# A two-layer decoder trunk: one plain pair of up-projections a layer in place of two, right factors at four steps a chunk, three buffers of weight parts, bias read later

## The chip, the cores and the metric

The kernel runs on one core of a Trainium2 chip. The metric is the device time of one execution in microseconds (us); lower is better. Names of engines in profiles: PE is TensorE, with PEld its weight loads; DVE is VectorE, ACT is ScalarE, POOL is GpSimd, and SP is SyncE, which issues the reads of weights. L345 is line 345 of the kernel.

## The reference

Input and output are 512 tokens by 1024 channels in float32. Layer 0 is a causal convolution module followed by a SwiGLU feed-forward network (FFN). After it keys and values are projected once. Layer 1 is sliding-window attention with a relative-position bias and its own FFN, and a last RMSNorm. The FFN, D_FF = 2816, is the larger part of the work:

```python
def rmsnorm(x, g):
    xf = x.astype(jnp.float32)
    xf = xf * lax.rsqrt(jnp.mean(xf * xf, axis=-1, keepdims=True) + EPS)
    return (xf * g.astype(jnp.float32)).astype(x.dtype)

def swiglu_ffn(x, w_up, w_down):
    gate, up = jnp.split(x @ w_up, 2, axis=-1)
    return (jax.nn.silu(gate) * up) @ w_down
```

## The kernel before

**Products.** Every float32 product is made from two shorter parts of each factor, a high half and a low half, with three matmuls (`mm3`): high by high (L345), high weights by the low half of the activation (L346), low weights by the high half (L347). `h[0..7]` holds the residual stream, 128 channels by 512 tokens in each tile.

**Weights.** They are read in chunks of 512 KB (128x1024) on SP's queue into four `raw` buffers, in the order of a list, `PLAN`, and up to six chunks ahead of their use. `split_chunk` then makes `whi` on ACT (a cast, L269) and `wlo` on VectorE (a subtraction, also L269), up to three chunks ahead, with four buffers of each. All of it happens in `get`, which is called once for each chunk that TensorE is to use.

**The FFN.** Its hidden width is cut into 11 pairs of 256 gate and 256 up columns. There are two ways to make a pair's up-projections:

- A *plain* pair (`ffn_up`): four chunks (two halves of the channels, gate and up), each with 24 matmuls of 128x512 into four PSUM banks. The activation is not yet divided by its root mean square. The row scales (`rsbc`) come in meanwhile: L434 sums squares on TensorE, VectorE makes the mean (L436), POOL takes the power (L438), L451 spreads the scales over the partitions on TensorE, and ACT copies them to SBUF (L444). Then `evac` multiplies two gate banks by the scales (L500, VectorE), applies silu (L501, ACT), multiplies two up banks (L502, VectorE), multiplies both (L503, POOL), and splits the result into a high half (L463, ACT) and a low half (L464, VectorE).
- A *product* pair (`ffn_prod`): seven products of half the width (Strassen's scheme over halves of channels and tokens), each with 24 matmuls of 128x256. It needs sums of weights (L227, L228, L231, L232, on VectorE, from a `blocks` tile of 3 x 1024 columns and two `raw` tiles) and seven *right factors*, sums of quarters of the normalised activation with a high and a low half each, made once a layer by `right_factors`: rows (L1013, VectorE), sums (L558, L559, L561, L570, VectorE), high halves (L532 and L535, ACT) and low halves (L533 and L536, VectorE).

The pairs are worked in parts (`HALVES0`, `HALVES1`): a part makes the hidden values of its pairs and then their down-projections, 24 matmuls of 128x512 a chunk and two chunks a pair. Part 0 holds the plain pairs, two of them, because products cannot start without right factors.

**What sets the order.** `get` also runs a generator in the background: at each chunk, `rate` steps of it. `factors` is such a generator: it lets four steps pass, asks for the row scales, and then makes the right factors step by step (`right_factors` yields twelve times). At the end of part 0 `flush` issues what is left. A scheduler then sets the order of each engine's instructions; engines work through theirs strictly in that order. Two buffers (`bufs=2`) of `blocks` serve both the pairs' weight parts and, while right factors are made, two tiles of these.

**The bias table** (16 heads by 256 columns by 128 partitions) is read by eight DMAs of 256 KB (L1000) just ahead of the layer 0 FFN; attention uses it after the keys and values.

Of the kernel before, what the change touches and what calls it, by code (L numbers as in the profile page):

```python
# [10 lines left out]
F32 = mybir.dt.float32  # L11
# [6 lines left out]
P = 128  # L18
# [7 lines left out]
NH = 16  # L26
# [6 lines left out]
N_WARM = 9  # L33
HALVES0 = ((0, 2), (2, 5), (5, 8), (8, 11))
HALVES1 = ((0, 2), (2, 6), (6, 9))
PLAIN = (2, 2)
LAST = (9, 11)
# [135 lines left out]
def hybrid_trunk(ctx: ExitStack, tc: tile.TileContext, xT, W, prm_in, wdw_in, rnd_in, sinks, relb, onehot, fin, out):  # L173
# [11 lines left out]
    def uid(s):  # L185
        ctr[0] += 1
        return f"{s}{ctr[0]}"
# [334 lines left out]

    def right_factors(row, x):

        tiles = [str_pool[0].tile([P, 3, 1024], F32, tag="blocks", name=uid("blocks")) for _ in range(2)]
        b = [[t[:, n] for n in range(2)] for t in tiles]
# [464 lines left out]
    attn = ExitStack()  # L991
    table_pool = attn.enter_context(tc.tile_pool(name="table", bufs=1))
    bias = table_pool.tile([P, NH, BAND], F32, tag="bias", name="bias", bufs=1)
    blocks = ExitStack()
    str_pool[0] = blocks.enter_context(tc.tile_pool(name="blocks", bufs=2))

# [6 lines left out]

    base = seen[0]
    job(read_bias(), (base + 6, 0), (base + 36, 9))

    def factors(gain, n, x):
        for _ in range(4):
            yield
        rs2 = n.rms.step2().rearrange("p (j s) -> p j s", j=2)  # L1010

        def row(i, dst):
            nc.vector.scalar_tensor_tensor(dst, h[i].rearrange("p (j s) -> p j s", j=2), col(gain, i), rs2,  # L1013
                                           op0=ALU.mult, op1=ALU.mult)

        yield from right_factors(row, x)

    def ffn_parts(layer, parts, n, on_h=None):
        gain = n.gains[0]
        right = {}  # L1020
        background.append(factors(gain, n, right))
        rate[0] = 1.5
        ffn_part(layer, 0, n.x[gain], n.rms)
        flush()
        rate[0] = 0
        for part in range(1, parts):
            ffn_part(layer, part, right, None, on_h if part == parts - 1 else None)
        return right
# [4 lines left out]
    if True:  # L1033
        ffn_parts(0, 4, n0, nxt.on_h)
        blocks.close()
        str_pool[0] = None
        at = attn.enter_context(tc.tile_pool(name="attn", bufs=2))
        x, rms = nxt.x, nxt.rms
# [174 lines left out]
    blocks = ExitStack()  # L1213
    str_pool[0] = blocks.enter_context(tc.tile_pool(name="blocks", bufs=2))

# [98 lines left out]
```

## Time and profile before

| | us |
|---|---|
| time, median of 3 runs | 1053.49 (1052.31 to 1053.57) |
| the profiled execution's own time | 1053.42 |
| its span, first to last instruction | 1051.6 |
| TensorE busy | 1039.6 (99%) |
| VectorE busy | 754.5 (72%) |
| ACT busy | 502.7 (48%) |
| POOL busy | 185.7 (18%) |
| mean granted clock of TensorE | 0.997 |

In rows of a timeline the first number is the start within the span in us, the second the duration from there (of all, where a row ends in x2 or more), then engine, line and operation, output<-inputs by the program's names, and shapes. Square brackets give how long the engine was idle before and what ended that. Instructions on an engine overlap a little, so the spacing of starts, not the duration, is what a row costs in a dense stretch. In rows of windows each engine has its busy time and its number of instructions, then come the granted clock of TensorE (1.00 is full), the busy share of the DMA engines and GB/s.

### The profile page before, as it was taken

What the parts mean: (1) busy time and instruction counts of PE and PEld (TensorE: products, weight loads), DVE (VectorE), ACT (ScalarE), POOL (GpSimd) and SP (SyncE); (2) the same over time, 40 slices, a digit from 0 to 9 for tenths busy, and PEclk for the clock granted to TensorE, in tenths of its full rate; (3) what the DMA queues carried; (4) which work ended last, traced back from release to release, by engine and by line L of the source; (5) the groups of instructions that cost most, each with busy time, mean ns of one, the idle gap of its engine ahead of it and who ended that gap; (6) DMA issues with size and microseconds to landing.
All of it is one profiled execution on the core that took longest, in us unless ns stands there. A gap on an engine that the chain in (4) does not pass through costs nothing.

```text
span 1051.6 us, 16101 instructions
## 1 busy us (share of the span) xinstructions
PE 1039.6 (99%) x6492; PEld 899.9 (86%) x6492; DVE 754.5 (72%) x981; ACT 502.7 (48%) x765; POOL 185.7 (18%) x200
## 2 busy tenths in 40 slices
PE   9999999999999999999999999999999999999997
PEld 7766568888998999899879878788899988998996
DVE  8799866599776587576684677578977754776663
ACT  6665745352552345155453766345355432542443
POOL 0799801311000000000130534041100000000000
PEclk9999999999999999999999999999999999999999
DMA  7766684323234124121323120232333431342112
GB/s 252 183 163 178 147 145 114 100 80 141 82 123 138 65 97 160 61 81 62 120 81 100 61 61 22 80 106 88 128 99 104 142 117 41 112 142 88 41 61 80
DMA packets 36934, 111.64 MB, mean 106 GB/s; under 512 B 4411, under 2 KB 7276, under 8 KB 36844
## 3 DMA queue, kind: packets, MB, share of 16 engines
q1 hardware_dynamic: 35708, 109.32, 34.6%
q10 hardware_dynamic: 1152, 1.29, 0.3%
q8 instruction: 51, 0.84, 0.3%
q14 instruction: 23, 0.19, 0.1%
HBM read 106.25 MB, written 4.73 MB: 106 GB/s over the span
## 4 chain that ended last, share of the span: by engine, by line
PE 94%; DVE 2%; DMA 2%; issue 1%; ACT 1%; SPq 0%; POOL 0%; POOLq 0%; ACTq 0%; DVEq 0%
PE bank L337 23%; PE bank L345 23%; PE bank L346 23%; PE bank L347 23%; PE bank L1243 2%; DMA shifted<-rowsd 1%; DVE quad L460 1%; DMA h<-in_xT_dram 0%; DVE wlo L269 0%; DMA rowsd<-apad 0%; PE bank L451 0%; PE bank L1233 0%; PE bank L434 0%; ACT whi L269 0%; DVE h L489 0%
## 5 line engine op out<-in xcount | busy, mean ns | idle before, releaser
L346 PE MATMUL bank<-quad,whi 128*128 128x256 f32 (+1 forms) x1536 | 488.4, 320 | 0.9 <-DVE quad L460 0.9
L345 PE MATMUL bank<-quad,whi 128*128 128x256 f32 (+1 forms) x1536 | 484.1, 321 | 0.4 <-ACT tmp L607 0.4
L347 PE MATMUL bank<-quad,wlo 128*128 128x256 f32 (+1 forms) x1536 | 482.5, 319 | 0.0
L269 ACT CAST whi<-raw 128x1024 fp32r<-128x1024 f32 x174 | 183.0, 1053 | 293.6 <-PE bank L346 197.4
L346 PEld LDWEIGHTS bank<-quad,whi 128*128 128x128 f32 x1536 | 292.5, 190 | 22.1 <-DVE quad L460 1.3
L345 PEld LDWEIGHTS bank<-quad,whi 128*128 128x128 f32 x1536 | 291.3, 190 | 22.9 <-issue 0.6
L347 PEld LDWEIGHTS bank<-quad,wlo 128*128 128x128 f32 x1536 | 290.0, 190 | 20.1
L269 DVE TENSOR_TENSOR wlo<-raw,whi 128x1024 fp32r<-128x1024 f32 x174 | 221.2, 1274 | 111.5 <-ACT whi L269 109.1
L337 PE MATMUL bank<-quad,whi 128*128 128x512 f32 x512 | 160.7, 395 | 1.3 <-DVE quad L280 0.8
L337 PEld LDWEIGHTS bank<-quad,whi 128*128 128x128 f32 x512 | 94.6, 188 | 27.1 <-issue 5.1
L269 DVE TENSOR_TENSOR wlo<-blocks,whi 128x1024 fp32r<-128x1024 f32 x54 | 65.6, 1224 | 57.2 <-ACT whi L269 57.2
L337 PE MATMUL bank<-quad,wlo 128*128 128x512 f32 x256 | 100.0, 391 | 0.1
L269 ACT CAST whi<-blocks 128x1024 fp32r<-128x1024 f32 x54 | 56.7, 1051 | 90.6 <-PE bank L346 71.3
L825 POOL TENSOR_TENSOR quad<-quad 128x512 f32<-128x512 f32 x53 | 75.7, 1428 | 12.4 <-ACT quad L823 9.3
L337 PEld LDWEIGHTS bank<-quad,wlo 128*128 128x128 f32 x256 | 48.0, 188 | 10.8 <-DVE wlo L280 0.6
L1254 POOL TENSOR_TENSOR rs<-ss,mhalf 128x1 f32<-128x1 f32 x4 | 2.2, 548 | 298.0 <-DVE ss L1252 298.0
L424 POOL TENSOR_TENSOR tmp<-tmp,tmp 128x512 f32<-128x512 f32 x21 | 32.8, 1564 | 112.7 <-ACT tmp L422 101.3
L1116 POOL COPY sc<-sk 128x4 f32<-128x4 f32 x16 | 3.5, 251 | 257.1 <-DVE wlo L269 254.9
L823 ACT ACTIVATE quad<-apad,wdw 128x512 f32<-128x512 f32 x53 | 36.9, 720 | 18.6 <-POOL quad L825 18.6
L489 DVE TENSOR_TENSOR h<-bank,h 128x512 f32<-128x512 f32 x56 | 37.1, 686 | 9.0 <-PE bank L347 9.0
L1140 POOL TENSOR_SCALAR sc<-sc,sm 128x256 f32<-128x256 f32 (+1 forms) x64 | 31.8, 515 | 66.0 <-DVE sm L1138 65.8
L1136 ACT ACTIVATE sc<-sc,m 128x257 f32<-128x257 f32 (+1 forms) x64 | 30.4, 479 | 22.1 <-DVE m L1127 22.1
(168 smaller groups left out, 1017.4 us busy)
## 6 DMA issues: line engine op xcount, KB each, us to landing
raw<-in_W_dram SPq DMA_DIRECT2D x139, 512.0 KB, 3.6
blocks<-in_W_dram SPq DMA_DIRECT2D x36, 512.0 KB, 4.4
shifted<-rowsd SPq DMA_DIRECT2D x16, 262.0 KB, 5.2
shifted<-rowsd SPq DMA_DIRECT2D x12, 260.0 KB, 5.7
rowsd<-apad SPq DMA_DIRECT2D x8, 271.0 KB, 2.7
bias<-fd SPq DMA_DIRECT2D x8, 256.0 KB, 10.2
shifted<-rowsd SPq DMA_DIRECT2D x4, 264.0 KB, 5.0
h<-in_xT_dram SPq DMA_DIRECT2D x4, 256.0 KB, 4.2
```

What stands on the lines that cost most here:

```text
L269: done = (nc.scalar.copy(hi, r).ins, lo_engine[0].tensor_sub(lo, r, f32(hi)).ins)
L337: turn[0] = nc.tensor.matmul(*args, **kw).ins
L345: nc.tensor.matmul(out, w[0], x[0], start=start, stop=False, **kw)
L346: nc.tensor.matmul(out, w[0], x[1], start=False, stop=False, **kw)
L347: nc.tensor.matmul(out, w[1], x[0], start=False, stop=stop, **kw)
L424: eng.tensor_add(sq, self.acc[eng], sq)
L489: nc.vector.tensor_add(t, banks[m], t)
L823: nc.scalar.mul(pr, src, self.tap(j))
L825: nc.gpsimd.tensor_add(to, acc, pr)
L1136: nc.scalar.activation(sc[:, j, 0:1 + w], sc[:, j, 0:1 + w], AF.Exp, bias=self.m4[:, j:j + 1], scale=-1.0, accum_out=sm[:, j:j + 1])
L1140: nc.gpsimd.tensor_scalar(sc[:, j, 1:1 + w], sc[:, j, 1:1 + w], sm[:, j:j + 1], 0.0, op0=ALU.mult, op1=ALU.add)
L1243: nc.tensor.matmul(self.banks[g], x, w[:, k, :], start=False, stop=kp == LAST[1] - 1 and k == 1 and n == 2)
```

## The change

One plain pair a layer instead of two (`PLAN` and the parts follow), so layer 0's parts hold 1, 3, 3 and 4 pairs in place of 2, 3, 3 and 3, and layer 1's hold 1, 4 and 4, in place of 2, 4 and 3, before the last two pairs. The generator of right factors runs at four steps a chunk in place of 1.5, after six steps that it lets pass in place of four; its two tiles are taken before it starts. `blocks` has three buffers in place of two. The bias table is allocated and read after the layer 0 FFN, in the memory that `blocks` gives back.

```diff
-HALVES0 = ((0, 2), (2, 5), (5, 8), (8, 11))
-HALVES1 = ((0, 2), (2, 6), (6, 9))
-PLAIN = (2, 2)
+HALVES0 = ((0, 1), (1, 4), (4, 7), (7, 11))
+HALVES1 = ((0, 1), (1, 5), (5, 9))
+PLAIN = (1, 1)
...
-    def right_factors(row, x):
-
-        tiles = [str_pool[0].tile([P, 3, 1024], F32, tag="blocks", name=uid("blocks")) for _ in range(2)]
+    def right_factors(row, x, tiles):
+
         b = [[t[:, n] for n in range(2)] for t in tiles]
...
     attn = ExitStack()
-    table_pool = attn.enter_context(tc.tile_pool(name="table", bufs=1))
-    bias = table_pool.tile([P, NH, BAND], F32, tag="bias", name="bias", bufs=1)
     blocks = ExitStack()
-    str_pool[0] = blocks.enter_context(tc.tile_pool(name="blocks", bufs=2))
+    str_pool[0] = blocks.enter_context(tc.tile_pool(name="blocks", bufs=3))
...
-    base = seen[0]
-    job(read_bias(), (base + 6, 0), (base + 36, 9))
-
-    def factors(gain, n, x):
-        for _ in range(4):
+    def factors(gain, n, x, tiles):
+        for _ in range(6):
             yield
...
-        yield from right_factors(row, x)
+        yield from right_factors(row, x, tiles)
...
-        background.append(factors(gain, n, right))
-        rate[0] = 1.5
+        tiles = [str_pool[0].tile([P, 3, 1024], F32, tag="blocks", name=uid("blocks")) for _ in range(2)]
+        background.append(factors(gain, n, right, tiles))
+        rate[0] = 4
...
         blocks.close()
         str_pool[0] = None
+        bias = attn.enter_context(tc.tile_pool(name="table", bufs=1)).tile([P, NH, BAND], F32, tag="bias", name="bias")
+        job(read_bias(), (seen[0] + 1, 0), (seen[0] + 5, 9))
...
     attn.close()
     blocks = ExitStack()
-    str_pool[0] = blocks.enter_context(tc.tile_pool(name="blocks", bufs=2))
+    str_pool[0] = blocks.enter_context(tc.tile_pool(name="blocks", bufs=3))
```

Lines move up by one from L525 and by three after L1000: L1013 is L1007 in the changed kernel, L532 and L533 are L531 and L532, L535 and L536 are L534 and L535, L558, L559, L561 and L570 are L557, L558, L560 and L569.

**How instructions move, layer 0** (layer 1 has the same order, but for a row or two). TensorE at the end of the up-projections, first before: `quad200` and `quad201` are high and low half of the activation, `quad227` and `quad228` those of the hidden values, whi264 and whi267 the last up chunk and the first down chunk.

```order
L347 MATMUL bank258_1808<-quad200_1468,wlo265_1846 128x512
L345 MATMUL bank258_1808<-quad200_1468,whi264_1845 128x512
L346 MATMUL bank258_1808<-quad201_1469,whi264_1845 128x512
L347 MATMUL bank258_1808<-quad200_1468,wlo265_1846 128x512
L345 MATMUL bank279_1964<-quad227_1641,whi267_1879 128x512
L346 MATMUL bank279_1964<-quad228_1642,whi267_1879 128x512
```

Here the hidden values at the fifth row are those of pair 0; 96 matmuls (pair 1's ups) stand between its last up matmul and this row. In the change (`quad229` and `quad230` are the hidden values):

```order
L347 MATMUL bank234_1644<-quad200_1464,wlo241_1680 128x512
L345 MATMUL bank260_1823<-quad229_1639,whi247_1729 128x512
L345 MATMUL bank261_1824<-quad229_1639,whi247_1729 128x512
L345 MATMUL bank262_1825<-quad229_1639,whi247_1729 128x512
L345 MATMUL bank263_1826<-quad229_1639,whi247_1729 128x512
L345 MATMUL bank268_1866<-quad229_1639,whi251_1767 128x512
L345 MATMUL bank269_1867<-quad229_1639,whi251_1767 128x512
L345 MATMUL bank270_1868<-quad229_1639,whi251_1767 128x512
L345 MATMUL bank271_1869<-quad229_1639,whi251_1767 128x512
L346 MATMUL bank260_1823<-quad230_1640,whi247_1729 128x512
```

The first row is the last up matmul of the only plain pair. Eight matmuls with the high half follow it, then one with the low half; all 48 down matmuls stand ahead of product 0.

VectorE behind the row scales (rsbc202), first before, from the fifth row behind them, the last of the first evacuation's multiplications, to the first low half of hidden values (`quad228`):

```order
L502 TENSOR_TENSOR tmp254_1798<-bank232_1646,rsbc202_1470 128x512
L269 TENSOR_TENSOR wlo265_1846<-raw242_1717,whi264_1845 128x1024
L558 TENSOR_TENSOR blocks249_1759<-blocks250_1760,blocks249_1759 128x1024
L464 TENSOR_TENSOR quad228_1642<-tmp252_1790,quad227_1641 128x512
L533 TENSOR_TENSOR quad262_1816<-blocks249_1759,quad262_1816 128x1024
```

In the change, from the same multiplication to the low halves (`quad230`); ahead of these rows stand the eight L1007, L500, L532, L269, L557, L532, L502, L500 and L231:

```order
L502 TENSOR_TENSOR tmp259_1816<-bank234_1644,rsbc202_1466 128x512
L558 TENSOR_TENSOR blocks227_1637<-blocks227_1637 128x1024
L269 TENSOR_TENSOR wlo273_1873<-raw246_1726,whi272_1872 128x1024
L560 TENSOR_TENSOR blocks227_1637<-blocks228_1638,blocks227_1637 128x1024
L232 TENSOR_TENSOR raw246_1726<-raw246_1726,raw239_1676 128x1024
L569 TENSOR_TENSOR blocks228_1638<-blocks227_1637,blocks228_1638 128x1024
L535 SCALAR_TENSOR_TENSOR quad253_1774<-blocks227_1637,quad253_1774 128x1024
L532 TENSOR_TENSOR quad254_1777<-blocks227_1637,quad254_1777 128x1024
L532 TENSOR_TENSOR quad255_1780<-blocks227_1637,quad255_1780 128x1024
L464 TENSOR_TENSOR quad230_1640<-tmp257_1808,quad229_1639 128x512
L464 TENSOR_TENSOR quad230_1640<-tmp259_1816,quad229_1639 128x512
```

Sums and low halves of right factors, and sums of weights, have moved ahead of the low half of the hidden values. On ACT, the change has the high half (L463) behind three casts of right factors, of which the first reads what VectorE's L560 writes:

```order
L501 ACTIVATE tmp258_1815<-tmp258_1815 128x512
L534 ACTIVATE quad253_1774<-blocks227_1637 128x1024
L531 CAST quad254_1777<-blocks227_1637 128x1024
L531 CAST quad255_1780<-blocks227_1637 128x1024
L463 CAST quad229_1639<-tmp257_1808 128x512
L463 CAST quad229_1639<-tmp259_1816 128x512
```

Before, the first L463 stands directly behind its L501, ahead of any cast of a right factor.

TensorE between the sums of squares (L434) and the spreading of the scales (L451), in the change:

```order
L434 MATMUL bank242_1683<-ones_c_103,tmp226_1634 128x1 x4
L346 MATMUL bank231_1641<-quad201_1465,whi236_1647 128x512
L347 MATMUL bank231_1641<-quad200_1464,wlo237_1648 128x512
L347 MATMUL bank232_1642<-quad200_1464,wlo237_1648 128x512
L345 MATMUL bank232_1642<-quad200_1464,whi236_1647 128x512
L346 MATMUL bank232_1642<-quad201_1465,whi236_1647 128x512
L347 MATMUL bank232_1642<-quad200_1464,wlo237_1648 128x512
L451 MATMUL bank245_1692<-ident_117,rs244_1690 128x128 x4
L345 MATMUL bank233_1643<-quad198_1462,whi221_1585 128x512
```

Six matmuls stand between the two; before there are 25. Behind L451 come the up columns' two chunks (whi221 and whi240), 48 matmuls.

## The prediction, made before the changed kernel ran

> **What bounds the kernel now.** I read the page first: the busy shares, then the chain of work that ended last.
>
> ```profile
> span 1051.6 us, 16101 instructions
> PE 1039.6 (99%) x6492; PEld 899.9 (86%) x6492; DVE 754.5 (72%) x981; ACT 502.7 (48%) x765; POOL 185.7 (18%) x200
> PE 94%; DVE 2%; DMA 2%; issue 1%; ACT 1%; SPq 0%; POOL 0%; POOLq 0%; ACTq 0%; DVEq 0%
> ```
>
> TensorE is busy for 99% of the span and is 94% of the chain. So there are two ways to change the time: fewer or shorter matmuls, or a wait that TensorE does not have now. The shares are averages, so I looked next at each engine in the stretch that the change rewrites, the first part of the layer 0 FFN: up-projections (192 to 237 us), down-projections (237 to 259), first products (259 to 300).
>
> ```profile
> core 0: us, PE busy (x) PEld busy (x) DVE busy (x) ACT busy (x) POOL busy (x), PEclk, DMA share, GB/s
> 192.00:237.00 45.00, 45.00 (x208) 37.49 (x207) 35.71 (x37) 20.81 (x26) 11.01 (x7) 1.00 0.26 82
> 237.00:259.00 22.00, 22.00 (x99) 18.23 (x98) 22.00 (x24) 6.07 (x7) 3.44 (x2) 1.00 0.40 144
> ```
>
> VectorE, 72% on the whole, is busy for all of the 22 us under the down-projections. It is the engine that is second here, and all right factors and both evacuations of the up-projections pass through it. Its timeline (start, duration, line) shows where that solid stretch begins:
>
> ```profile
> 210.39 1.23 DVE L269 TENSOR_TENSOR wlo<-raw,whi 128x1024 fp32r<-128x1024 f32 x1 [5.17 <-ACT whi L269]
> 211.53 2.73 DVE L1013 SCALAR_TENSOR_TENSOR blocks<-h,prm,rsbc 128x512 f32<-128x512 f32 x4
> 214.18 0.69 DVE L500 TENSOR_TENSOR tmp<-bank,rsbc 128x512 f32<-128x512 f32 x1
> 214.78 2.73 DVE L1013 SCALAR_TENSOR_TENSOR blocks<-h,prm,rsbc 128x512 f32<-128x512 f32 x4
> 219.22 1.42 DVE L269 TENSOR_TENSOR wlo<-raw,whi 128x1024 fp32r<-128x1024 f32 x1
> 220.56 2.31 DVE L558 TENSOR_TENSOR blocks<-blocks,blocks 128x1024 f32<-128x1024 f32 x1
> 225.67 1.21 DVE L533 TENSOR_TENSOR quad<-blocks,quad 128x1024 fp32r<-128x1024 f32 x1
> 226.81 1.21 DVE L269 TENSOR_TENSOR wlo<-raw,whi 128x1024 fp32r<-128x1024 f32 x1
> 238.29 2.03 DVE L269 TENSOR_TENSOR wlo<-raw,whi 128x1024 fp32r<-128x1024 f32 x1
> 243.11 1.78 DVE L464 TENSOR_TENSOR quad<-tmp,quad 128x512 fp32r<-128x512 f32 x1
> 247.08 0.68 DVE L464 TENSOR_TENSOR quad<-tmp,quad 128x512 fp32r<-128x512 f32 x1
> ```
>
> From 211.5 us on there is no idle time in front of any row. The second plain pair's hidden values have their low halves only at 243.11 and 247.08 us, after TensorE has begun the down-projections at 237.42 (row below). Nothing waits, because TensorE first multiplies pair 0's hidden values. That cover is what the change takes away.
>
> **The change part by part.** *The swapped pair.* Rows of TensorE's timeline, the first down matmul and the first two products of the next part:
>
> ```profile
> 237.42 0.39 PE L345 MATMUL bank<-quad,whi 128*128 128x512 f32 x1
> 259.18 0.28 PE L345 MATMUL bank<-quad,whi 128*128 128x256 f32 x1
> 261.81 0.28 PE L346 MATMUL bank<-quad,whi 128*128 128x256 f32 x1
> ```
>
> Between the first two stand 96 matmuls of 512 columns: 21.76 / 96 = 0.2267 us each, 5.44 us a chunk of 24. Between the second and third stand 22 of 256 columns: 0.1195 us each. A plain pair's ups (96 x 0.2267 = 21.76) become seven products (168 x 0.1195 = 20.08). Gain 1.68 us a layer, 3.36 in both.
>
> *Who covers the evacuation now.* The order of the change (shown above) puts all 48 down matmuls of the one plain pair directly behind its last up chunk and ahead of product 0. I count from the end of the copy of the row scales (L444), since VectorE's L1007 (L1013 before) and L500 all need it:
>
> ```profile
> 210.61 0.59 ACT L444 COPY rsbc<-bank 128x512 f32<-128x512 f32 x1 [0.25 <-PE bank L451]
> 209.52 1.05 PE L451 MATMUL bank<-ident,rs 128*128 128x128 f32 x8
> 210.33 0.48 PE L346 MATMUL bank<-quad,whi 128*128 128x512 f32 x1
> ```
>
> The copy ends at 211.20, 0.87 us after TensorE goes on from L451. In the change exactly two up chunks follow L451, 10.88 us, so TensorE wants the hidden values at +10.0.
>
> VectorE works in its order. From +0 to the end of L560 stand eight 128x512 L1007 at 0.66 us (two groups above: 2.65 from 211.53 to 214.18 for four), four L500/L502 at 0.60 (214.18 to 214.78) and eight 128x1024 rows at 1.135 (225.67 to 226.81): 5.3 + 2.4 + 9.1 = +16.8. On ACT, the hidden high half (L463) stands behind L534, which waits for that L560, and two L531. Their rows:
>
> ```profile
> 229.79 1.06 ACT L535 ACTIVATE quad<-blocks 128x1024 fp32r<-128x1024 f32 x1 [2.18 <-DVE blocks L561]
> 230.76 2.93 ACT L532 CAST quad<-blocks 128x1024 fp32r<-128x1024 f32 x3
> 244.38 0.62 ACT L463 CAST quad<-tmp 128x512 fp32r<-128x512 f32 x1 [0.45 <-POOL tmp L503]
> ```
>
> 0.97 + 2 x 0.94 + 0.62, and about 0.1 for the hand-over: high half at +20.35. TensorE waits 10.35 us. It then has eight matmuls that need only the high half (1.81 us, to +22.15); the low half (L464) comes after five more 1.135 us rows on VectorE and its own 0.68: +23.15. Another 1.0. Base stall: **11.35 us**.
>
> *Two additions.* In the rows above, those beside a POOL multiplication L503 are long: L558 2.31 for 1.21, L269 2.03 and 1.42 for 1.21, L464 1.78 for 0.68; two of POOL's rows at those times:
>
> ```profile
> 218.26 3.54 POOL L503 TENSOR_TENSOR tmp<-tmp,tmp 128x512 f32<-128x512 f32 x2 [12.16 <-DVE tmp L502]
> 242.19 2.15 POOL L503 TENSOR_TENSOR tmp<-tmp,tmp 128x512 f32<-128x512 f32 x1 [2.96 <-DVE tmp L502]
> ```
>
> That is 1.10 + 0.21 + 0.82 + 1.10 = 3.2 us for four, 0.8 each. The plain pair's two L503 now fall between the copy and L560: +1.6 (bounds 0, where they meet rows that read a bank, and 2.2). The second is TensorE's clock when it resumes. It is seen once, before the layer 0 FFN, in windows of 1 us:
>
> ```profile
> 142.00:143.00 1.00, 0.75 (x7) 0.66 (x7) 0.48 (x3) 0.99 (x1) 0.00 (x0) 1.00 0.00 0
> 144.00:145.00 1.00, 0.90 (x5) 0.90 (x6) 0.49 (x1) 0.00 (x0) 0.05 (x1) 0.73 1.06 204
> 145.00:146.00 1.00, 1.00 (x6) 1.00 (x5) 0.08 (x1) 0.00 (x0) 0.00 (x0) 0.50 1.16 115
> 146.00:147.00 1.00, 1.00 (x2) 0.35 (x2) 1.00 (x2) 0.36 (x1) 0.00 (x0) 0.50 1.19 130
> 147.00:148.00 1.00, 1.00 (x2) 0.34 (x1) 0.89 (x2) 0.97 (x2) 0.00 (x0) 0.57 1.18 101
> 546.00:553.00 7.00, 6.10 (x32) 4.89 (x31) 6.73 (x8) 3.92 (x6) 2.17 (x2) 1.00 0.22 76
> ```
>
> After some 10 us of small matmuls with gaps the clock fell to 0.5 and cost 0.27 + 0.5 + 0.5 + 0.43 = 1.7 us; a stretch with 0.9 us of idle in 7 did not lower it. A stall of 12 us is far nearer the first. Of the 1.7, 1.0 hides in the wait for the low half: +0.7 (bounds 0 and 1.7). I take both: 11.35 + 1.6 + 0.7 = **13.65 us a layer**.
>
> The Trainium skill, "TensorE: Matmul & The Clock Gate", Part 1 ("What's actually happening"), says that TensorE falls back to half clock after an idle window of about 3.4 us and needs about as long a busy one to recover; by it each stall here is followed by half clock, and without it the sum would be 1.4 us lower. The trace agrees on the half and on some 3.4 us of it, but not on the cause: in 141 to 144 us TensorE was busy for three quarters of the time, with no such idle window.
>
> *Scales nearer to their sums.* Before, 25 matmuls stand between L434 and L451; now 6 (7 in layer 1).
>
> ```profile
> 202.90 0.95 PE L434 MATMUL bank<-ones_c,tmp 128*128 128x1 f32 x8
> 203.71 0.49 PE L345 MATMUL bank<-quad,whi 128*128 128x512 f32 x1
> 204.13 1.97 POOL L438 TENSOR_TENSOR rs<-ms,mhalf 128x4 f32<-128x4 f32 x1 [6.14 <-DVE ms L436]
> ```
>
> POOL's power ends at 206.10, 2.39 us after TensorE goes on; six matmuls cover 1.36. Wait 1.0, in layer 1 0.8 (bounds 0 and 1.2 each). What is queued behind L451 is TensorE itself, and the copy, so this delays the whole count above, not only part of it.
>
> *A sum of weights earlier.* The third buffer lets the first product pair's parts be read before the FFN, and their first sum (L227, 1.135 us) now stands on VectorE inside the chain at the end of the convolution (L280), shortly ahead of this row:
>
> ```profile
> 148.34 0.69 DVE L280 TENSOR_TENSOR quad<-tmp,quad 128x512 fp32r<-128x512 f32 x1 [0.41 <-ACT tmp L280]
> ```
>
> VectorE idles 0.41 us there, so up to 0.7 of the 1.135 is late, and TensorE needs this quad. I take 0.4 in layer 0, and 0.3 in layer 1, where the sum stands between rows of the output projection (bounds 0, if it falls in an idle stretch, and 1.5, the sum and a late read).
>
> *The bias table and the read-ahead.* The table's pieces now go on SP's queue behind the layer 0 FFN's last weights.
>
> ```profile
> bias<-fd SPq DMA_DIRECT2D x8, 256.0 KB, 10.2
> raw<-in_W_dram SPq DMA_DIRECT2D x2, 512.0 KB, 6.0
> ```
>
> A read of weights behind them lands 6.0 us after its issue; the last part's eight down chunks (8 x 5.44 = 43.5 us) lie over it. Nothing at the end; without that cover a few us. VectorE's product work after the stall is the same rows as before, and only its order changes: 0.
>
> *Sum*, against the profiled execution's own 1053.42 us (span 1051.6 and 1.8 around it; the median of the runs, 1053.49, is the same to 0.07): layer 0, 0.4 + 1.0 + 13.65 - 1.68 = +13.4; layer 1, 0.3 + 0.8 + 13.65 - 1.68 = +13.1. 1053.4 + 26.5 = **1080**.
>
> **The rivals.** *The evacuation is in time.* This is the side of a gain. If the hidden values are ready by +10.0, both stalls vanish, and with the small terms at their lower bounds 1053.4 - 3.4 = **1050**. For it speaks that the ups of one pair are only half as much to evacuate. Against it: what lies ahead is not the evacuation but the right factors, 5.3 + 9.1 us of VectorE rows against 10.0. It decides from the point where the rows ahead of L464 sum to less than about 9 us, so they would have to take under half of what they did.
>
> *ACT does not hold the high half.* If the hidden high half came as soon as its own inputs do (L502 at about +11, one L503 1.3, one cast 0.62: +13) and the low half 2.5 us behind, the stall is 5.5 and each layer gains or loses 5.5 + 1.2 - 1.7 = +5: **1064**. Against it stands the order on ACT.
>
> *More than the stall.* The table's pieces delay the key and value weights, or the waits for high and low half give two slow stretches of the clock a layer, 1.7 each: **1084 to 1090**. For it: a piece takes 10.2 us and eight are issued together.
>
> *Nothing to be told.* Gains and stall near each other, **1053**, which needs a stall of under 2 us.
>
> **How the numbers follow.** Stall as summed 0.78, held less on ACT 0.07, more than the stall 0.07, in time 0.05, nothing 0.03. With every lower bound the likeliest gives 11.35 - 1.68 and 0.0 to 0.3 a layer, 1073; with every upper bound 1.5 + 1.2 + 11.35 + 2.2 + 1.7 - 1.68 = 16.3 a layer, 1086. Its own range is 1073 to 1086; to take in half of the neighbours' weight I go down to 1066 and up to 1087. A measurement of this kernel can tell about 0.2%, 2.1 us, from no change: slower by more than that 0.92, within 0.03, faster 0.05.
>
> **What would show it.** In the profile of the changed kernel, TensorE idles about 10 to 12 us just ahead of the first 512-column matmul of the downs, with L463 or the ACT cast behind L560 as releaser; a second short wait for L464 eight matmuls later; the granted clock near 0.5 for some 3 us in between; TensorE's busy time about 3 us lower but the span 25 longer; a wait of about 1 us at L451. All of it twice, once a layer. If TensorE runs through into the downs, the step on the cover is wrong; if the idle is there but 5 us, the step on ACT's order is; if the clock stays at 1.00, the 0.7 is.

## The result, and the profile after

The changed kernel takes **1086.76 us** (median of 4 runs, 1085.09 to 1087.6) against 1053.53 for the kernel before: a ratio of 1.0312 [1.03, 1.0324], 33 us slower. The prediction was 1080, with a range of 1066 to 1087. The sum below goes by the two profiled executions, 1087.6 us (span 1085.8) after and 1053.42 (span 1051.6) before, so 34.2 us are to be found.

The page of the changed kernel: span, busy times and the chain that ended last.

```profile
span 1085.8 us, 16415 instructions
PE 1043.8 (96%) x6636; PEld 906.7 (84%) x6636; DVE 771.9 (71%) x997; ACT 508.9 (47%) x777; POOL 176.7 (16%) x196
PE 85%; DVE 6%; ACT 2%; POOL 2%; issue 2%; DMA 2%; SPq 0%; POOLq 0%; ACTq 0%; DVEq 0%
```

TensorE's share of the chain fell from 94% to 85%, and VectorE's rose from 2% to 6%: TensorE now waits on work that VectorE ends last. Its busy time is 4 us longer, although it has less to multiply; the clock, below, is part of why: at half clock TensorE loses 4.8 us in the two layers, where the kernel before lost 1.7 in all. TensorE's waits say where it stands still (releaser, us in total, times, longest):

```profile
PE bank L345 <- ACT quad L463: 24.8, 2, 12.5
PE bank L345 <- ACT tmp L606: 3.2, 11, 0.4
PE bank L346 <- DVE quad L280: 1.8, 1, 1.8
```

The first is one wait of 12.4 us a layer, for the cast of the hidden values' high half. The second is a product that waits for a copy out of a bank, eleven times. Before, the same copy (L607 there) held TensorE once:

```profile
PE bank L345 <- ACT tmp L607: 0.4, 1, 0.4
```

Now the place of the first wait in layer 0, on the changed kernel's timeline: TensorE, then VectorE, ACT and POOL.

```profile
205.79 1.16 PE L451 MATMUL bank<-ident,rs 128*128 128x128 f32 x8
...
230.24 3.78 PE L345 MATMUL bank<-quad,whi 128*128 128x512 f32 x8 [12.37 <-ACT quad L463]
233.82 0.63 PE L346 MATMUL bank<-quad,whi 128*128 128x512 f32 x1
...
219.65 1.98 DVE L231 TENSOR_TENSOR raw<-blocks,raw 128x1024 f32<-128x1024 f32 x1
223.29 2.28 DVE L269 TENSOR_TENSOR wlo<-raw,whi 128x1024 fp32r<-128x1024 f32 x1
225.49 1.21 DVE L560 TENSOR_TENSOR blocks<-blocks,blocks 128x1024 f32<-128x1024 f32 x1
232.30 1.28 DVE L464 TENSOR_TENSOR quad<-tmp,quad 128x512 fp32r<-128x512 f32 x2
...
206.98 0.59 ACT L444 COPY rsbc<-bank 128x512 f32<-128x512 f32 x1
226.74 1.06 ACT L534 ACTIVATE quad<-blocks 128x1024 fp32r<-128x1024 f32 x1 [6.33 <-DVE blocks L560]
227.70 1.98 ACT L531 CAST quad<-blocks 128x1024 fp32r<-128x1024 f32 x2
229.58 1.13 ACT L463 CAST quad<-tmp 128x512 fp32r<-128x512 f32 x2
...
219.28 1.27 POOL L503 TENSOR_TENSOR tmp<-tmp,tmp 128x512 f32<-128x512 f32 x1 [13.55 <-DVE tmp L502]
222.38 2.11 POOL L503 TENSOR_TENSOR tmp<-tmp,tmp 128x512 f32<-128x512 f32 x1 [1.83 <-DVE tmp L502]
```

The first product of L503 ends at 220.6 and the second at 224.5, but the two casts that need them begin only at 229.6 and 230.1, and TensorE goes on when the first of these is done. In between ACT stands in front of L534 for 6.33 us, because L534 reads what VectorE's L560 writes from 225.49 to 226.70. When TensorE resumes, its eight matmuls take 3.58 us (230.24 to 233.82) in place of 1.81. The windows show why; the column behind POOL's is the granted clock.

```profile
219.00:231.00 12.00, 0.76 (x2) 0.66 (x3) 12.00 (x11) 4.89 (x7) 3.38 (x2) 0.59 0.00 0
221.00:222.00 1.00, 0.00 (x0) 0.00 (x0) 1.00 (x2) 0.00 (x0) 0.00 (x0) 0.63 0.00 0
231.00:234.00 3.00, 3.00 (x9) 2.32 (x8) 3.00 (x5) 1.61 (x2) 0.00 (x0) 0.50 0.30 41
234.00:235.00 1.00, 1.00 (x4) 0.79 (x3) 1.00 (x2) 0.00 (x0) 0.00 (x0) 0.55 0.74 291
```

VectorE is busy all the time in which TensorE does nothing. The clock falls in the window from 221 to 222 (0.63 is 1.00 up to 221.3 and 0.50 from there) and is back at 234.9 (0.55): 3.4 us behind the end of TensorE's last matmul (217.9), and 4.7 us after it goes on at 230.24. The Trainium skill, "TensorE: Matmul & The Clock Gate", Part 1 ("What's actually happening"), has TensorE at half clock after an idle window of about 3.4 us until it has been busy for about as long; by that rule the trace agrees here on the fall, and on the return roughly, with 4.7 us of matmuls at half clock behind a wait of 12.4.

### The profile page after: what moved, and what is told of

It is laid out like the page before. It is cut to its first block, busy times and chain, and to the rows that moved or that the text cites. A ratio compares the mean times of both kernels' runs of the same rounds, so it can differ in the third digit from the quotient of the medians.

```text
span 1085.8 us, 16415 instructions
## 1 busy us (share of the span) xinstructions
PE 1043.8 (96%) x6636; PEld 906.7 (84%) x6636; DVE 771.9 (71%) x997; ACT 508.9 (47%) x777; POOL 176.7 (16%) x196
## 4 chain that ended last, share of the span: by engine, by line
PE 85%; DVE 6%; ACT 2%; POOL 2%; issue 2%; DMA 2%; SPq 0%; POOLq 0%; ACTq 0%; DVEq 0%
PE bank L345 22%; PE bank L346 21%; PE bank L347 21%; PE bank L337 18%; POOL quad L824 2%; PE bank L1240 2%; DVE wlo L269 1%; DVE blocks L1007 1%; DVE quad L460 1%; ACT whi L269 1%; DMA shifted<-rowsd 1%; DMA raw<-in_W_dram 1%; DMA rowsd<-apad 0%; DMA blocks<-in_W_dram 0%; DVE raw L231 0%
## 5 line engine op out<-in xcount | busy, mean ns | idle before, releaser
L345 PE MATMUL bank<-quad,whi 128*128 128x256 f32 (+1 forms) x1584 | 492.7, 318 | 28.0 <-ACT quad L463 24.8
L346 PE MATMUL bank<-quad,whi 128*128 128x256 f32 (+1 forms) x1584 | 496.0, 315 | 2.7 <-DVE quad L280 1.8
L347 PE MATMUL bank<-quad,wlo 128*128 128x256 f32 (+1 forms) x1584 | 489.6, 314 | 0.0
L345 PEld LDWEIGHTS bank<-quad,whi 128*128 128x128 f32 x1584 | 302.6, 192 | 51.6 <-ACT quad L463 25.7
L269 ACT CAST whi<-raw 128x1024 fp32r<-128x1024 f32 x174 | 182.4, 1050 | 306.1 <-PE bank L346 206.7
L346 PEld LDWEIGHTS bank<-quad,whi 128*128 128x128 f32 x1584 | 302.5, 191 | 22.2 <-DVE quad L280 2.2
L347 PEld LDWEIGHTS bank<-quad,wlo 128*128 128x128 f32 x1584 | 299.6, 191 | 17.9
L269 DVE TENSOR_TENSOR wlo<-raw,whi 128x1024 fp32r<-128x1024 f32 x174 | 221.6, 1276 | 117.0 <-ACT whi L269 112.4
L337 PEld LDWEIGHTS bank<-quad,whi 128*128 128x128 f32 x512 | 94.7, 188 | 27.9 <-issue 5.1
L269 DVE TENSOR_TENSOR wlo<-blocks,whi 128x1024 fp32r<-128x1024 f32 x60 | 73.0, 1220 | 60.8 <-ACT whi L269 60.8
L269 ACT CAST whi<-blocks 128x1024 fp32r<-128x1024 f32 x60 | 62.9, 1048 | 90.7 <-PE bank L346 66.2
L337 PEld LDWEIGHTS bank<-quad,wlo 128*128 128x128 f32 x256 | 48.1, 188 | 10.9 <-DVE wlo L280 0.6
L822 ACT ACTIVATE quad<-apad,wdw 128x512 f32<-128x512 f32 x53 | 36.8, 718 | 18.7 <-POOL quad L824 18.7
L228 DVE TENSOR_TENSOR blocks<-raw,blocks 128x1024 f32<-128x1024 f32 x20 | 26.7, 1333 | 20.9 <-DMA raw<-in_W_dram 20.6
## 6 DMA issues: line engine op xcount, KB each, us to landing
bias<-fd SPq DMA_DIRECT2D x8, 256.0 KB, 10.1
```

Of the source, the lines that this page charges most:

```text
L228: nc.vector.tensor_add(b21, a11, b21)
L269: done = (nc.scalar.copy(hi, r).ins, lo_engine[0].tensor_sub(lo, r, f32(hi)).ins)
L337: turn[0] = nc.tensor.matmul(*args, **kw).ins
L345: nc.tensor.matmul(out, w[0], x[0], start=start, stop=False, **kw)
L346: nc.tensor.matmul(out, w[0], x[1], start=False, stop=False, **kw)
L347: nc.tensor.matmul(out, w[1], x[0], start=False, stop=stop, **kw)
```

## The experiments

The theory at this point: the second plain pair was TensorE's work while VectorE made right factors, and without it nothing covers them. Rivals: the cost comes from the rest of the change (order, buffers, late bias); or only from the order in which evacuation and right factors stand; or largely from the clock. All kernels are timed against the kernel before on the same chip (1053.68 to 1054.12 there).

**1. Everything but the swap.** The parts are cut as before, with two plain pairs a layer; rate, buffers and bias stay as in the change.

```diff
-HALVES0 = ((0, 1), (1, 4), (4, 7), (7, 11))
-HALVES1 = ((0, 1), (1, 5), (5, 9))
-PLAIN = (1, 1)
+HALVES0 = ((0, 2), (2, 5), (5, 8), (8, 11))
+HALVES1 = ((0, 2), (2, 6), (6, 9))
+PLAIN = (2, 2)
```

> Two plain pairs a layer as before, with everything else of the change (four steps a chunk, six steps let pass, three buffers of weight parts, late bias). If the stall comes from the missing second pair (my theory), there is no wait of 12 us ahead of the downs; what is left is the wait of about 1.8 us at the end of the convolution and perhaps the short waits in the products: 1054 to 1057 us. If the faster right factors are the cause whatever covers them, the stall stays: 1075 to 1088 us. If the third buffer causes the short waits inside the products (3 to 5 us in all in the changed kernel), they show here too: 1058 to 1061.

Measured: 1058.51 us, 1.0044 [1.0029, 1.0059]. The largest of TensorE's waits in it:

```profile
PE bank L345 <- ACT tmp L606: 2.6, 9, 0.4
```

The long wait is gone, so the swap makes it. The short ones are there without the swap; the time is 4.8 us above the kernel before.

**2. The same with two buffers of weight parts.** Only `bufs` of `blocks` goes back, beside the cut of run 1.

```diff
-    str_pool[0] = blocks.enter_context(tc.tile_pool(name="blocks", bufs=3))
+    str_pool[0] = blocks.enter_context(tc.tile_pool(name="blocks", bufs=2))
```

> The run with two plain pairs and everything else of the change, but with two buffers of weight parts as before. If the third buffer is what brought its 4.8 us (the short waits of TensorE for the copy L606 at the border of two product pairs), they are gone: 1052.5 to 1055 us. If the four steps a chunk or the late bias brought them, they stay: 1057 to 1060.

Measured: 1053.99 us, 1.0005 [0.9996, 1.0015], no change from the kernel before. Its waits for L606:

```profile
PE bank L345 <- ACT tmp L606: 0.4, 1, 0.4
```

So the third buffer brings the short waits, and with two plain pairs rate 4, the six steps that pass and the late bias cost nothing together. One of these waits in run 1, TensorE and then ACT:

```profile
290.42 0.28 PE L347 MATMUL bank<-quad,wlo 128*128 128x256 f32 x1
291.05 0.39 PE L345 MATMUL bank<-quad,whi 128*128 128x256 f32 x1 [0.35 <-ACT tmp L606]
...
289.46 1.05 ACT L269 CAST whi<-blocks 128x1024 fp32r<-128x1024 f32 x1 [2.97 <-issue]
290.41 0.58 ACT L606 COPY tmp<-bank 128x512 f32<-128x512 f32 x1
```

Product 4 writes the bank that product 2 filled, so L606 must have emptied it. On ACT, L606 stands behind a cast of weights; both together take 1.53 us (289.46 to 290.99). The cover is what TensorE has left of product 3 behind product 2, since the two are worked into each other. In this product pair the scheduled order has 10 matmuls of product 3 behind the end of product 2 in run 1 (10 x 0.12 = 1.2 us), and 22 in run 2 (2.6 us). The wait and the restart cost 0.51 us (0.63 between the first two rows in place of 0.12); eight more of them are 4.1 us of the 4.5 between runs 1 and 2. The count bears this out: in the scheduled orders of the kernel before, the changed one and runs 1 and 2, the product pairs that have only 10 or 11 matmuls there number 1, 11, 9 and 1, which is also how often each of them waits for this copy. Why one more buffer makes the scheduler interleave the products otherwise was not followed up.

**3. Evacuation ahead of the right factors.** The generator makes nothing under the up-projections; it is run out right behind the evacuation.

```diff
         hid = ffn_prod(layer, lo, hi, xg) if rms is None else ffn_up(layer, lo, hi, xg, rms)
+        if rms is not None:
+            flush()
...
-        rate[0] = 4
+        rate[0] = 0
```

> The changed kernel, with the right factors issued after the evacuation of the plain pair, so that on VectorE the four multiplications by the row scales, and on ACT the high half, stand ahead of all sums and parts. If the order on ACT and VectorE makes the stall (my theory), the high half comes about 3.5 us after the ups and the low half some 5 us later: stall 8 in place of 14.6 a layer, about 1073 us. If VectorE's total work between scales and products sets the time whatever its order, the wait only moves to the products: 1084 to 1088.

Measured: 1082.67 us, 1.028 [1.026, 1.03]: 4 us of the 33 come back, not 14. TensorE's waits:

```profile
PE bank L345 <- ACT quad L463: 9.1, 2, 4.6
PE bank L346 <- DVE quad L464: 7.4, 2, 3.9
PE bank L347 <- DVE wlo L269: 3.0, 3, 1.6
```

The wait for the high half falls from 12.4 to 4.5 us, as it would if order were the cause. But VectorE's work has only changed places: the low half (3.5 to 3.9 us) and then the products' weights (1.5) are late in its stead. The clock takes the rest, in layer 0 on TensorE and in the windows:

```profile
221.35 3.78 PE L345 MATMUL bank<-quad,whi 128*128 128x512 f32 x8 [4.54 <-ACT quad L463]
228.64 0.79 PE L346 MATMUL bank<-quad,whi 128*128 128x512 f32 x1 [3.51 <-DVE quad L464]
...
221.00:225.00 4.00, 3.65 (x8) 2.48 (x8) 4.00 (x6) 1.68 (x3) 1.32 (x1) 0.50 0.01 4
225.00:229.00 4.00, 0.49 (x2) 0.36 (x2) 4.00 (x6) 1.32 (x2) 0.00 (x0) 0.50 0.00 0
```

In layer 0 the clock is at 0.50 from 219.5 to 233.1 us, 13.65 us as in the changed kernel, but 8.3 us of matmuls fall into that time in place of 4.7, and each takes twice as long. In layer 1, behind the same two waits, it is low for 3.4 us twice, with 6.4 us of matmuls. So this order recovers little. It is not a test of order alone: with nothing made under the ups, the scales are spread behind the last of them (L451 at 215.76, 48 matmuls behind the sums), so that the evacuation starts later too. The evacuation first with early scales was not run.

**4. The old pace of the generator.** One plain pair, but 1.5 steps a chunk after four that pass.

```diff
-        for _ in range(6):
+        for _ in range(4):
...
-        rate[0] = 4
+        rate[0] = 1.5
```

> The changed kernel with 1.5 steps a chunk after four that it lets pass, as before. On ACT the first high half then stands ahead of all casts of right factors, on VectorE the low halves behind fewer rows, but L451 comes 26 rows after L434 and leaves only 4.4 us of ups behind the copy. My theory (what stands ahead of the hidden values in the fixed orders makes the stall): about 5.5 us for the high half and 2 for the low, clock 1 to 2, so 1071 to 1079. If the stall is a matter of the missing cover alone, whatever the order: 1085 to 1090.

Measured: 1081.7 us, 1.0262 [1.0245, 1.028]. Again the stall is divided, not removed:

```profile
PE bank L345 <- ACT quad L463: 11.1, 2, 5.6
PE bank L347 <- DVE wlo L269: 5.9, 2, 3.4
```

5.6 us a layer stand ahead of the downs, and 3.4 in layer 0 and 2.6 in layer 1 at the third product (product 2), for a low half of its weights (L269) that VectorE now makes later. The time lies between the two ranges that had been expected.

**5. The wait filled with other matmuls.** 44 matmuls, whose results nothing reads, stand between ups and downs, so that TensorE is not idle for long. All that the reference needs is still computed.

```diff
+    def fill(xg):
+        pb = bank()
+        for n in range(44):
+            nc.tensor.matmul(pb, xg[0][0][:, 0:P], xg[n % 8][0], start=n == 0, stop=n == 43)
...
+            fill(xg)
             evac(pair, banks)
```

> The changed kernel with 44 matmuls of 128x512 (10 us at full clock, of operands at hand, their result unused) put on TensorE between the ups and the downs, inside the wait. If the half clock after the wait costs time (my theory: 2.3 us a layer, of which 1.0 comes back as the wait for the low half), the clock stays at 1.00 and the time falls by 2 x 1.3 to about 1084 us. If the clock costs nothing beyond waits that are there anyway: 1086 to 1088. If the added matmuls themselves delay the downs: above 1088.

Measured: 1084.1 us, 1.0287 [1.0272, 1.0303]. The eight matmuls with the high half, and the one behind them in layer 0; then the eight in layer 1:

```profile
228.44 2.12 PE L345 MATMUL bank<-quad,whi 128*128 128x512 f32 x8 [2.49 <-ACT quad L463]
231.23 0.50 PE L346 MATMUL bank<-quad,whi 128*128 128x512 f32 x1 [0.67 <-DVE quad L464]
...
745.26 3.44 PE L345 MATMUL bank<-quad,whi 128*128 128x512 f32 x8 [2.56 <-ACT quad L463]
```

In layer 0 they run at full clock. From the last up matmul to the twelfth down matmul 1.1 us come back, not all that the clock had cost, because at full clock TensorE reaches the low half before it is ready and waits 0.67 us there. In layer 1 the clock still falls, from 745.7 to 749.1 us, behind a wait of only 2.56 us, and 0.6 us come back. So the time came out as expected, but not for the reason expected: the clock gives some 1.7 of the 2.7 us, and the other 1.0 fits two short waits in the products fewer (nine for eleven, 0.51 each). 44 matmuls (10 us) that cost nothing show how large the hole is.

**6. Products in the hole.** If cover is what lacks, useful work should fill it. Products 0 and 1 of the next pair go between the ups and the downs of the plain pair. Right factors for them are made before the evacuation, and the spreading of the scales is asked for behind 12 matmuls of the third up chunk. In this kernel and the next four, L352, L353, L354 (or L357 and on, L363 and on) are the old L345 to L347.

```diff
-                plan.extend(("prod", layer, pair, j) for j in range(7))
+                for j in range(7):
+                    if pair == PLAIN[layer] and j == MID:
+                        plan.extend(("down", layer, kp, g) for g in range(2) for kp in range(PLAIN[layer]))
+                    plan.append(("prod", layer, pair, j))
...
-                nc.vector.tensor_mul(t2, banks[2 + m], rs_bc)
+                with tc.issue_after(los[0]) if m else nullcontext():
+                    nc.vector.tensor_mul(t2, banks[2 + m], rs_bc)
...
+            mid(2)
             product(2, a, False, False)
```

> One plain pair a layer, but products 0 and 1 of the next pair stand between its ups and its downs, the right factors that these two need are issued ahead of the evacuation and the others behind it, and TensorE spreads the row scales 12 matmuls after their sums. If cover is all that was missing (my theory), the stall shrinks to 1 to 2 us a layer: 1053.5 - 3.0 for the swapped pairs + 1.8 at the convolution + 3 + the products' short waits (0 to 5) = 1054 to 1060 us. If VectorE cannot make the right factors in that time, product 2 waits in place of the downs: 1065 to 1085.

Measured: 1072.67 us, 1.018 [1.0163, 1.0197]. TensorE, layer 0:

```profile
216.78 0.28 PE L352 MATMUL bank<-quad,whi 128*128 128x256 f32 x1
218.87 0.39 PE L352 MATMUL bank<-quad,whi 128*128 128x256 f32 x1 [1.82 <-ACT quad L558]
223.63 2.50 PE L352 MATMUL bank<-quad,whi 128*128 128x512 f32 x5 [4.37 <-ACT quad L470]
```

The expectation failed in its size. The second of the two products' 48 matmuls, the first of product 1, waits 1.82 us for the high half of its right factor. Directly behind it the scheduled order has five down matmuls (the x5 row), ahead of the other 46 product matmuls, so the downs are not behind the products as intended, and the wait for the hidden high half is still 4.37 us. 14 of the 33 us come back.

**7. Downs held behind product 1, weights' sums later.** The downs may start only behind the last matmul of product 1; the first sums of weights (L227, L228) wait for the first update of `h`.

```diff
-            nc.vector.tensor_add(s1, b21, b22)
-            nc.vector.tensor_add(b21, a11, b21)
+            with tc.issue_after(sums_after[0]) if sums_after[0] is not None else nullcontext():
+                nc.vector.tensor_add(s1, b21, b22)
+                nc.vector.tensor_add(b21, a11, b21)
...
-                    downs(layer, 0, PLAIN[layer], first[0])
+                    with tc.issue_after(last_mm[0]):
+                        downs(layer, 0, PLAIN[layer], first[0])
```

> As the run with two products between ups and downs, with the downs held behind product 1 on TensorE, and the first sum of weights held behind the convolution's first update of h. The waits of 4.4 and 1.9 us (for the high half by a down matmul put too early, and at the convolution) go, with the slow clock behind them: 1072.7 - 2 x (4.6 + 1.8) - 1.6 = 1058, less 1 to 3 for the wait at product 0. With three buffers the short waits in the products stay. 1055 to 1060 us.

Measured: 1071.24 us, 1.0165 [1.015, 1.0181]. Its largest waits:

```profile
PE bank L358 <- DVE quad L564: 6.5, 4, 2.6
PE bank L357 <- ACT quad L563: 3.6, 2, 1.8
```

The expectation failed by 11 us. The wait for the hidden values is gone, and that at the convolution's end (L280 before the FFN) is down to 0.4 us. What is late now are the right factors of the first two products: the high half (L563) for the first matmul of product 1, which stands second, and the low halves (L564) behind it. It is the same VectorE and ACT work, seen from another place. The clock is at 0.50 for 6.8 us a layer around these waits, in this run as in runs 6 and 8, and 3.7 to 4.7 us of matmuls fall into it, so that it takes about 2 us a layer besides the waits.

**8. Two buffers, one right-factor tile apart.** Run 2 had shown the price of the third buffer, so the weight parts have two and one tile of right factors gets its own.

```diff
-        tiles = [str_pool[0].tile([P, 3, 1024], F32, tag="blocks", name=uid("blocks")) for _ in range(2)]
+        tiles = [str_pool[0].tile([P, 3, 1024], F32, tag=tag, name=uid("blocks"), bufs=n) for tag, n in (("right", 1), ("blocks", 2))]
...
-    str_pool[0] = blocks.enter_context(tc.tile_pool(name="blocks", bufs=3))
+    str_pool[0] = blocks.enter_context(tc.tile_pool(name="blocks", bufs=2))
```

> The same with two buffers of weight parts, of which the right factors' second tile uses one, and a buffer of its own for their first tile. If the third buffer of weight parts makes the short waits in the products, they go too: 1053.5 - 3.0 for the pairs + 1 to 2 at product 0 = 1051 to 1054 us. If not, as the run beside it: 1055 to 1060.

Measured: 1067.91 us, 1.0143 [1.012, 1.0165]. The waits for the copy out of the bank are down from seven to one, and 3.3 us are gone with them; the time is still above both expected ranges, by 8 us or more, because the waits for the right factors stay as they were. That for the low halves:

```profile
PE bank L358 <- DVE quad L564: 6.3, 4, 2.6
```

**9. Scales spread in time.** In runs 6 to 8 the spreading of the scales stood 25 rows behind the sums on TensorE, whatever had been asked. Here the rest of that up chunk and the fourth are held behind it; the down weights' low halves on VectorE go behind the right factors, and those of products 2 and on behind the hidden values.

```diff
-                        hold = half == 1 and which == 0 and (k, m) == order[AT2 + 1] and pair == lo
+                        hold = pair == lo and half == 1 and (which == 1 or order.index((k, m)) > AT2)
...
+        if PLAN[i][0] == "down" and PLAN[i][2] < PLAIN[PLAN[i][1]]:
+            wait = (los[PLAN[i][3]],)
+        if PLAN[i][0] == "prod" and PLAN[i][2] == PLAIN[PLAN[i][1]] and PLAN[i][3] >= MID:
+            wait = (los["hid"],)
```

> As the run with the right factors' tile apart, with the scales really spread 12 matmuls behind the sums (all later ups are held behind L451), the downs' low weights behind the right factors of products 0 and 1, the rest of the right factors behind the last multiplication by the scales, and the weights of product 2 behind the hidden low halves. By the rows' durations the ups end 7.3 us after the copy; product 0 has its low half at 7.1, product 1 at 10.3 (wanted at 10.2), the downs theirs at 13.8 and a POOL multiplication or two later (wanted at 13.1). If that sum holds: 1 to 2.5 us of waits a layer against 1.5 gained, 1052 to 1056 us. If waits move to product 2 or to the clock: 1057 to 1065.

Measured: 1064.02 us, 1.0095 [1.0079, 1.0111], the best with one plain pair, and in the range of the second case, "if waits move". Its largest waits in the two FFNs:

```profile
PE bank L365 <- DVE wlo L285: 2.5, 2, 1.3
PE bank L364 <- DVE quad L572: 1.8, 2, 0.9
PE bank L364 <- DVE quad L569: 1.8, 2, 0.9
PE bank L363 <- ACT whi L285: 1.6, 2, 0.8
PE bank L363 <- ACT tmp L650: 1.3, 3, 0.8
```

There is no long wait left. These sum to 9.0 us, a restart of each not counted, and the swap gives 3.0; that is 6.0 of the 9.9 us by which this run is slower, and the rest was not followed up.

**10. The rest of the right factors earlier.** As run 9, but the generator is run out behind the second right factor, not behind the last multiplication of the evacuation.

```diff
-        with tc.issue_after(los["t2"]):
+        with tc.issue_after(los[1]):
             flush()
```

> The same, but the rest of the right factors already behind the low half of product 1's, so that two sums stand ahead of the hidden low halves on VectorE, and product 2's right factors ahead of most updates of h. One to two microseconds more wait at the downs than the run beside it, none at product 2: 1053 to 1058 us.

Measured: 1065.19 us, 1.0117 [1.0089, 1.0145], not to be told from run 9, and above the 1053 to 1058 expected. The wait moves once more, to low halves of weights (L285) and of the hidden values (L482):

```profile
PE bank L365 <- DVE wlo L285: 5.2, 2, 2.6
PE bank L364 <- DVE quad L482: 2.6, 2, 1.3
```

No version with one plain pair came near the kernel before. The swap by itself, with nothing else of the change, was not tried: with two buffers, the first product pair's weight parts and the tiles of right factors would wait for each other. Nor was the third buffer tried in the kernel before, where it does not fit beside the bias table that is read early.

## Why the prediction was right, and where its sum was not

The direction, the mechanism and both places were right; 7.7 us of the sum were missing. That the time still lies in the range is in part luck: 1086.76 is 0.2 us below its upper end, above the 1073 to 1086 of the likeliest case itself, and inside the band of the rival "more than the stall" (1084 to 1090), neither of whose causes occurred (nothing waits for the table, and there is one slow stretch of the clock a layer, not two). The measured column goes by TensorE's first matmuls of each stage in the two traces.

| step | predicted, us | measured, us |
|---|---|---|
| swapped pair, both layers | -3.36 | -3.02 |
| stall, clock and scales, layer 0 | 1.0 + 13.65 | 14.94 |
| stall, clock and scales, layer 1 | 0.8 + 13.65 | 15.13 |
| a sum of weights earlier, both layers, with 0.2 elsewhere | 0.7 | 2.0 |
| product work after the stall | 0 | 5.14 |
| sum | 26.5 | 34.2 |

*The swapped pair.* A product pair takes 20.25 us, not 20.08: 1.51 us a layer gained. Right to 0.2.

*Who covers the evacuation.* Right, and run 1 shows it. The count from the copy's end gave the high half at +21.95 with POOL's share; it came at +22.6, and TensorE waited 12.37 us, where 11.95 had been counted. The step on ACT's order was right too: the first L463 stood behind L534 and two L531, though its L503 had ended 9 us earlier. Run 3 adds what the rival "ACT does not hold the high half" had left out. It put the low half 2.5 us behind the high half and counted no half clock; the low half was 3.5 us late on top of eight matmuls at half clock, and the weights of the products were late behind that. Its 1064 is 18.7 us below what run 3 took.

*The two additions.* The rows beside the two L503 took 1.98 and 2.28 for 1.21, 1.84 us in all for 1.6. The clock was sized too low: the eight matmuls lost 1.77 us and the next three about 0.5. None of that hid in the wait for the low half, as 1.0 had been taken to. L464 began at 232.30 and was done before the eight ended at 233.82. But then the 1.0 for that wait falls away as well, so that 2.3 stand against 1.7 for both. Run 5 has the clock by itself in layer 0, 1.1 us net.

*Scales nearer to their sums.* Wrong, by 1.0 us a layer in layer 0 and 0.8 in layer 1 too much. POOL's power took 1.02 us, where the one row of before had 1.97:

```profile
204.72 1.02 POOL L438 TENSOR_TENSOR rs<-ms,mhalf 128x4 f32<-128x4 f32 x1 [4.24 <-DVE ms L436]
```

The row of before was long because of what ran beside it on VectorE, a subtraction for a low half of weights that had begun 0.13 us earlier and ended at 205.23:

```profile
204.00 1.23 DVE L269 TENSOR_TENSOR wlo<-raw,whi 128x1024 fp32r<-128x1024 f32 x1
```

In the changed kernel VectorE idles in that time in both layers. Each of the twelve traces has three such powers behind 200 us (L438, or the line that it became): they take 1.96 to 1.98 us wherever such a subtraction has just begun, and 1.02 or 1.03 wherever VectorE is idle. The prediction had taken over a row that had run in other company. In the change the power ended at 205.74, and L451 began at 205.79, directly behind the six matmuls: no wait to speak of. This made up for the underestimate in the wait and the clock, so the two lines of the table agree better than their terms do.

*A sum of weights earlier.* The mechanism was right and its size off: 1.8 us in layer 0 for 0.4, none in layer 1 for 0.3. VectorE, ahead of the multiplication that TensorE needs (L280), in the changed kernel:

```profile
148.76 1.23 DVE L227 TENSOR_TENSOR blocks<-blocks 128x1024 f32<-128x1024 f32 x1 [0.83 <-DMA blocks<-in_W_dram]
149.90 0.68 DVE L280 TENSOR_TENSOR tmp<-tmp,bank 128x512 f32<-128x512 f32 x1
```

The sum waits 0.83 us for its read, with the rest of VectorE's queue behind it. The upper bound, "the sum and a late read", was the case, and at 1.5 it was a little short. Whether the read is late goes, in the traces compared here, with the clock just ahead of it. In the trace of before the clock falls to 0.50 from 144.5 to 147.9 us. In the changed kernel's it does not: that trace is 1.3 us behind at 137 us, has got 1.2 back by 148 us, and then finds the read late. Runs 3 and 4, with the same rows on VectorE and the fall of the clock, do not wait for the read, and TensorE's wait is 0.4 and 0.8 us; run 6, without the fall, waits 0.90 us for the read and 1.9 on TensorE. So the 0.2 elsewhere is a balance that holds these 1.2 us; another execution can have less of the wait and none of the gain.

*"VectorE's product work after the stall ... only its order changes: 0".* This is the step that failed: it cost 5.1 us. The prediction looked only at the order around the first part, and took the rest of the FFN as it was. But the third buffer changes the order in the product parts. Before, 12 to 22 matmuls of product 3 (22 are 2.6 us, 14 are 1.7) lay over the 1.53 us of cast and copy in all pairs but one, which had 10, and there was one wait of 0.4 us in the whole kernel; now it is 10 or 11 (1.2 or 1.3) in 11 of 20 product pairs, and there are eleven waits. Ten more at 0.51 us are the 5.1. Runs 1 and 2 settle that the buffer, not the swap, does it.

*The bias table.* Right: its pieces land 10.1 us after their issue (median) and no wait stands against them; in run 2, with the bias as late, nothing is lost.

## What to carry to other kernels

Before a piece of TensorE's work is removed because a cheaper form exists, find what other engines do under it: here 1.5 us a layer were gained on the matmuls and some 15 lost, because VectorE is busy without a gap under the removed work (21 of 21 us from 216 to 237 us in the kernel before), and each order tried only chose which of its results was late. A margin of a tenth of a microsecond that repeats with every tile (1.53 us of work under 1.7) belongs in the sum of any change that may touch the scheduled order, also far from the place of the edit; compare the order of the whole kernel, not that of the rewritten stage. Breaking a stall into shorter ones can bring back less than it seems, since the clock can stay low across all of them, as in layer 0 of run 3.

## What had not been expected of the hardware

- Half clock came in stretches of few lengths: by the granted clock of the twelve traces each one ahead of the last matmul lasts 3.4, 6.8 or 13.65 us. What it costs depends on how much of TensorE's work falls into it: 4.7 us of matmuls in layer 0 of the changed kernel and 8.3 in layer 0 of run 3, of the same 13.65. The length of a wait does not foretell it: in run 5 a wait of 2.49 us was followed by no half clock and one of 2.56 by 3.4 us of it.
- VectorE and POOL delay each other here, and the one that starts second is long. Two VectorE rows of 128x1024 with two inputs that began beside a running L503 took 1.98 and 2.28 us for 1.21 in the changed kernel. L558, which began 0.2 us ahead of the second L503, took its 1.21, and that L503 took 2.11 us, the first 1.27. POOL's power on 128x4, begun 0.13 us behind a VectorE subtraction, took 1.97 us for 1.02. One row is a bound only for the company that it ran in.
- In run 9 it was a right factor's low half that took 2.01 us beside a POOL multiplication (217.63 to 218.93 us), the one for which TensorE then waits 0.9 us a layer (L569 among its waits), so a contention of two engines that are not the bound reached the one that is:

```profile
218.01 2.01 DVE L569 TENSOR_TENSOR quad<-blocks,quad 128x1024 fp32r<-128x1024 f32 x1
```
